# Gate and up tiles from seven half-size products, and the residual summed in DRAM

## The chip, the cores and the metric

The program runs on one core of one Trainium2 chip. The metric is the device time of one execution in microseconds, as the median of several runs. The engines are named as in the profile: PE is TensorE (PEld its weight loads), DVE is VectorE, ACT is ScalarE, POOL is GpSimd, and SP is the engine that issues most DMAs.

## The reference

An encoder of two layers works on 768 tokens (a prompt of 512 and a sample of 256) with 1024 features. Each layer has three parts: a SwiGLU, a mixer (windowed attention and a long convolution), and a second SwiGLU. Each part is modulated by a conditioning vector `c` and closed by a layer norm. Cut to what matters here:

```python
mod = (silu(c) @ ada_w[l] + ada_b[l]).reshape(B, 9, 1024)
h = x * (1 + mod[:, 1]) + mod[:, 0]
g, u = split(h @ wi, 2)                  # wi: 1024 x 5632
f = (silu(g) * u) @ wo                   # wo: 2816 x 1024
x = layer_norm(ALPHA * x + 0.5 * (1 + mod[:, 2]) * f)
```

There are four SwiGLU parts in all: parts 0 and 2 of layer 0 and parts 0 and 2 of layer 1.

## The kernel before

Features lie on the 128 partitions and tokens run along the free axis, so an activation is a set of tiles of 128 features by 768 tokens. Every product is made of three matmuls in fp32r: the operand is split into a high part (a ScalarE copy that rounds) and a low part (a VectorE subtraction), and high x high, high x low and low x high are added up in PSUM (`mm3`, line 393). Weights are split on the fly. They come in units of 128 x 1024 (eight blocks of 128 x 128) in the fixed order of `w_units`: `w_load` (206) issues SP's DMA, `w_ahead` (213) has ScalarE write the high part and VectorE the low part of the next units, up to n ahead, and `w_take` (225) hands the next unit out.

The order of work on each engine is the order of the program text: the schedule is written by hand, an engine runs its instructions in that order, and each instruction waits for its operands and for its output buffer. Buffers come from fixed sets of slots (line 120): `slot_s` for activations, `slot_w` for split weights (6), `slot_r` and `slot_q` for raw weights, `slot_t` for temporaries (6), and eight PSUM banks.

A SwiGLU part (`swiglu`, 570) goes like this. The 2816 hidden features are 22 tiles j, each with a gate unit and an up unit. The first three j (six units) are made in the head, `Proj.head` (422), which overlaps with the layer norm of the part before (`final`, 505; `Norm.apply`, 354): the sample's columns first, then the prompt's. In part 0, where nothing is before, they are plain units. Then `rest` (593) makes j = 3 to 21 one after the other with `one` (598): `Proj.unit` (412) runs, for each of the two units, 24 matmuls of 512 columns and 24 of 256; `done` (578) applies Silu to the gate, multiplies it with the up tile on VectorE and splits the result into an `a` tile. The hidden tiles are consumed in six chunks. After the j named in `UNTIL`, the first four chunks of four hidden tiles each are multiplied with `wo` for all eight output tiles d in `out_step` (480), and VectorE adds each result to the residual x in SBUF. The last two chunks are run by `sample_out` (486) and `final`, interleaved with the norm.

```python
def out_step(o, x, coef, d):
    bp, bs = bank(), bank()
    o.d([(bp[:, :LP], 0), (bs[:, :LS], 1)], d)
    for s, b in ((0, bp[:, :LP]), (1, bs[:, :LS])):
        stt(x(d, SEQ[s]), b, coef[:, d, s:s + 1], x(d, SEQ[s]), ALU.mult, ALU.add)
```

A background generator, `ada_steps` (633), makes the modulation vectors from `ada_w`. One call of `pump(1)` (237) makes one tile: two VectorE passes over 128 x 1024, one for each sequence, and a DMA for a later tile. It runs in layer 0 alone: 56 tiles from the start of part 0, and 72 from the end of the head of part 2. `one` pumps two tiles per j in part 0 and three in part 2; the out steps pump one (part 0) or two (part 2) every second d.

The residual is written to DRAM (`x_spill`) only ahead of a mixer, which reads it back (`spill` in `finish`, `reload` in `attention`, 1333).

## Time and profile before

| | |
|---|---|
| median of 3 runs | 3071.99 us (3071.22 to 3072.28) |
| the profiled execution | 3068.34 us |
| its span, first to last instruction | 3066.5 us |
| mean granted clock of TensorE over the span | 0.989 |
| TensorE busy | 2988.5 us, 97% |
| TensorE weight loads busy | 2611.0 us, 85% |
| VectorE busy | 1754.6 us, 57% |
| ScalarE busy | 985.1 us, 32% |
| GpSimd busy | 456.9 us, 15% |
| DMA | 288.11 MB, mean 94 GB/s |

The profile shows one execution. A line of its timeline has the start in us from the span's start, the duration, the engine, the line of the kernel, the operation, the tiles written and read, their shape, the number of instructions merged into the line, and in brackets the idle time before it with what ended it. All instructions of this kernel go through one helper line (L70), so they are told apart by their tiles and shapes. Matmuls overlap: the duration of one record is longer than the distance between two starts.

### The profile page before, as it was taken

What the parts mean: (1) busy time and instruction counts of PE and PEld (TensorE: products, weight loads), DVE (VectorE), ACT (ScalarE), POOL (GpSimd) and SP (SyncE); (2) the same over time, 40 slices, a digit from 0 to 9 for tenths busy, and PEclk for the clock granted to TensorE, in tenths of its full rate; (3) what the DMA queues carried; (4) which work ended last, traced back from release to release, by engine and by line L of the source; (5) the groups of instructions that cost most, each with busy time, mean ns of one, the idle gap of its engine ahead of it and who ended that gap; (6) DMA issues with size and microseconds to landing.
All of it is one profiled execution on the core that took longest, in us unless ns stands there. A gap on an engine that the chain in (4) does not pass through costs nothing. (4 is left out here: it accounts for less than half of the span.)

```text
span 3066.5 us, 42447 instructions
## 1 busy us (share of the span) xinstructions
PE 2988.5 (97%) x17380; PEld 2611.0 (85%) x17380; DVE 1754.6 (57%) x3064; ACT 985.1 (32%) x1677; POOL 456.9 (15%) x459
## 2 busy tenths in 40 slices
PE   9999999999899999999999999999989999999998
PEld 3788888888888888888888888888888888888888
DVE  5565655567868667788273333325786873233326
ACT  3521112234367522111243111213426752211223
POOL 2400000034432400000040000003443240000002
PEclk9999999999999999999999999999999999999999
DMA  5433333323121145445121111112312111111111
GB/s 200 179 138 138 114 134 124 110 79 121 57 89 42 35 151 172 172 162 175 63 69 54 62 65 62 62 63 76 124 62 69 56 42 62 63 63 66 65 63 56
DMA packets 78571, 288.11 MB, mean 94 GB/s; under 512 B 11223, under 2 KB 14504, under 8 KB 75689
## 3 DMA queue, kind: packets, MB, share of 16 engines
q1 hardware_dynamic: 74680, 258.83, 24.8%
q0 software_dynamic: 3696, 26.58, 2.3%
q8 instruction: 136, 2.23, 0.3%
q14 instruction: 59, 0.48, 0.0%
HBM read 267.55 MB, written 17.83 MB: 93 GB/s over the span
## 5 line engine op out<-in xcount | busy, mean ns | idle before, releaser
L70 PE MATMUL bank<-slot_s,slot_w 128*128 128x512 f32 (+1 forms) x15000 | 2613.4, 336 | 20.2 <-DVE slot_s L70 15.8
L70 PEld LDWEIGHTS bank<-slot_s,slot_w 128*128 128x128 f32 x15000 | 2301.4, 191 | 320.3 <-DVE slot_s L70 21.5
L70 DVE TENSOR_TENSOR slot_w<-slot_r,slot_w 128x1024 fp32r<-128x1024 f32 x282 | 344.8, 1227 | 424.5 <-ACT slot_w L70 424.4
L70 ACT ACTIVATE slot_w<-slot_r 128x1024 fp32r<-128x1024 f32 x316 | 327.2, 1049 | 296.1 <-DMA slot_r<-w_units 244.4
L70 DVE SCALAR_TENSOR_TENSOR slot_s<-bank,tiny,slot_s 128x256 f32<-128x256 f32 (+1 forms) x416 | 238.9, 595 | 202.0 <-PE bank L70 201.9
L70 DVE CUSTOM_DVE_ANT_0 slot_t<-slot_q,slot_q 128x1024 bf16<-128x1024 f32 x256 | 310.8, 1222 | 28.1 <-DMA slot_q<-ada_t 17.3
L70 ACT ACTIVATE slot_t<-bank 128x512 f32<-128x512 f32 (+2 forms) x206 | 103.9, 505 | 679.9 <-PE bank L70 670.0
L70 DVE TENSOR_TENSOR slot_t<-slot_t,bank 128x256 f32<-128x256 f32 (+1 forms) x280 | 151.1, 540 | 272.6 <-PE bank L70 263.5
L70 ACT ACTIVATE slot_s<-slot_t 128x512 fp32r<-128x512 f32 (+1 forms) x220 | 114.8, 529 | 588.6 <-DVE slot_t L70 583.4
L70 POOL COPY slot_t<-slot_s 128x256 f32<-128x256 f32 (+1 forms) x13 | 6.6, 508 | 1984.7 <-DVE slot_s L70 1473.8
L70 DVE TENSOR_TENSOR slot_s<-slot_t,slot_s 128x256 fp32r<-128x256 f32 (+1 forms) x278 | 180.2, 650 | 118.7 <-ACT slot_s L70 104.1
L70 PE MATMUL bank<-slot_w,slot_s 128*128 128x256 f32 x864 | 107.6, 285 | 0.0
L70 PEld LDWEIGHTS bank<-slot_w,slot_s 128*128 128x128 f32 x864 | 105.5, 193 | 0.0
L70 POOL TENSOR_TENSOR slot_t<-slot_t,slot_s 128x256 f32<-128x256 f32 (+1 forms) x91 | 94.5, 1038 | 66.2 <-DVE slot_s L70 61.7
L70 ACT ACTIVATE slot_t<-slot_s 128x256 f32<-128x256 f32 (+1 forms) x132 | 65.6, 509 | 106.2 <-DVE slot_s L70 97.8
L70 POOL TENSOR_TENSOR slot_w<-slot_r,slot_w 128x1024 fp32r<-128x1024 f32 x34 | 81.5, 2399 | 119.4 <-ACT slot_w L70 100.8
L70 PE MATMUL bank<-slot_w,slot_w 128*128 128x256 f32 (+1 forms) x384 | 71.6, 342 | 20.4 <-ACT slot_w L70 14.8
L70 PEld LDWEIGHTS bank<-slot_w,slot_w 128*128 128x128 f32 x384 | 61.0, 215 | 30.1 <-ACT slot_w L70 17.4
L70 DVE TENSOR_TENSOR slot_t<-slot_t,slot_t 128x256 f32<-128x256 f32 (+3 forms) x120 | 78.6, 655 | 6.1 <-ACT slot_t L70 3.9
L70 ACT ACTIVATE slot_w<-slot_w,tiny 128x256 f32<-128x256 f32 (+1 forms) x144 | 74.4, 535 | 9.9 <-DVE tiny L70 9.6
L70 POOL TENSOR_SCALAR slot_s<-slot_t,lnp 128x256 f32<-128x256 f32 (+1 forms) x80 | 59.4, 743 | 83.4 <-DVE slot_t L70 83.0
L70 ACT ACTIVATE slot_s<-slot_t,tiny,tiny 128x256 fp32r<-128x256 f32 (+1 forms) x80 | 56.4, 704 | 46.9 <-DVE slot_t L70 46.9
(120 smaller groups left out, 1459.4 us busy)
## 6 DMA issues: line engine op xcount, KB each, us to landing
slot_r<-w_units SPq DMA_DIRECT2D x316, 512.0 KB, 3.5
slot_q<-ada_t SPq DMA_DIRECT2D x128, 512.0 KB, 3.6
slot_q<-ada_nat SPq DMA_DIRECT2D x16, 512.0 KB, 4.5
g_main<-slot_s POOLq DMA_DIRECT2D x4, 1536.0 KB, 8.7
x_spill<-slot_s POOLq DMA_DIRECT2D x4, 1536.0 KB, 7.0
slot_s<-g_main SPq DMA_DIRECT2D x4, 1536.0 KB, 7.2
slot_s<-x_spill POOLq DMA_DIRECT2D x4, 1536.0 KB, 7.1
slot_s<-x_in SPq DMA_DIRECT2D x2, 1536.0 KB, 9.0
```

Of the source, the lines that this page charges most:

```text
L70: return getattr(real, name)(*args, **kwargs)
```

## The change

The pairs j = 3 to 21 are made in another way. Take a pair's raw weights as a 2 x 2 block matrix: rows are input features 0 to 511 and 512 to 1023, columns are gate and up. Take the activations as 2 x 2 blocks too: the feature halves by tokens 0 to 383 and 384 to 767. The eight block products become seven (the scheme of Strassen and Winograd), each of a sum of weight blocks and a sum of activation blocks, and their results are combined by additions. Each product is 4 x 3 matmuls of 384 columns.

- The class `Fast` replaces `one`. `mid`, called inside the head ahead of the results of the prompt's first four banks (in part 0 after unit 3), makes the activation sums on GpSimd and VectorE, splits them, and loads the raw weights of j = 3. `begin` copies one more sum into h and prepares the first pair. `period` makes one pair and prepares the next.
- `sums` forms four weight sums per pair on GpSimd; per pair seven weight blocks of 128 x 512 are split (`prep_a` to `prep_d`), where it were four (two units of 128 x 1024).
- One bank collects four products; ScalarE copies it between products.
- The raw weights of a fast pair are loaded into a `slot_w`; the rest keep the old path with its own order (`_plan`) and a limit up to which `w_ahead` may split.
- `out_step` becomes `out_add`: ScalarE scales the two banks into a temporary, and a GpSimd DMA adds that to the residual in DRAM. The residual is in `x_spill` from the start of each SwiGLU part (for the first by a DRAM copy of `x_in`) and is read back ahead of the last two chunks.
- `slot_q` and `slot_r` become one set of seven, `slot_s` has ten, and the DMA descriptor scratch is set to 4096.

```diff
-SLOTS = {"slot_s": 9, "slot_w": 6, "slot_r": 3, "slot_q": 4, "slot_t": 6, "bank": 8, "tiny": 12}
+SLOTS = {"slot_s": 10, "slot_w": 6, "slot_r": 7, "slot_t": 6, "bank": 8, "tiny": 12}
...
     def w_ahead(n):
-        while w_state["split"] < min(w_state["next"] + n, n_units):
+        while w_state["split"] < min(w_state["next"] + n, w_state["limit"]):
...
-            w_load(i + 3)
+            w_load(i + w_state["raws"])
...
+            if self.mid is not None:
+                self.mid()
             w_ahead(2)
...
-    def out_step(o, x, coef, d):
+                w_ahead(min(self.ahead, self.room - len(self.ws)))
+    def out_add(o, coef, d):
         bp, bs = bank(), bank()
         o.d([(bp[:, :LP], 0), (bs[:, :LS], 1)], d)
+        v = slot_t([T])
         for s, b in ((0, bp[:, :LP]), (1, bs[:, :LS])):
-            stt(x(d, SEQ[s]), b, coef[:, d, s:s + 1], x(d, SEQ[s]), ALU.mult, ALU.add)
+            act.activation(out=v[:, SEQ[s]], in_=b, func=AF.Copy, scale=coef[:, d, s:s + 1])
+        gp.dma_start(x_spill[:, d, :], v, accum_op=ALU.add)
...
             for ci, chunk in enumerate(CHUNKS):
                 last = ci + 1 == len(CHUNKS)
-                while nj[0] < UNTIL[ci]:
-                    one()
+                while fast.j < UNTIL[ci]:
+                    fast.period(ci < 4 and fast.j + 1 == UNTIL[ci])
                 if coef is None:
                     coef = coef_of(l, 3 * which + 2, 0.5 / ALPHA)
                 o = Out([(a_of(j)[:, 0], a_of(j)[:, 1]) for j in chunk])
                 if ci + 2 >= len(CHUNKS):
+                    if not os:
+                        xn = Feat()
+                        for i in range(2):
+                            gp.dma_start(xn.more(i), x_spill[:, 4 * i:4 * i + 4, :])
+                        w_state["limit"], w_state["raws"] = w_stops.pop(0), 3
                     o.room = 6 - sum(before.n for before in os)
                     os.append(o)
                     if last:
                         drain()
-                        return end(os, x, coef)
+                        return end(os, xn, coef)
                     continue
+                w_state["limit"], o.ahead = w_state["next"] + len(chunk), 1
                 for d in range(ND):
-                    out_step(o, x, coef, d)
+                    out_add(o, coef, d)
...
+        def mid(self):
+            hh, hl = self.hh, self.hl
+            self.tt = {n: slot_s([4, 2, HT], F32R) for n in (2, 3, 4)}
+            self.t1 = slot_s([4, HT])
+            for d in range(4):
+                fa, fb, v = slot_t([2, HT]), slot_t([2, HT]), slot_t([2, HT])
+                al = slice(0, T)
+                tt(fa.rearrange("p a b -> p (a b)"), f32(hh(d, al)), f32(hl(d, al)), ALU.add, eng=gp)
+                tt(fb.rearrange("p a b -> p (a b)"), f32(hh(d + 4, al)), f32(hl(d + 4, al)), ALU.add, eng=gp)
+                tt(self.t1[:, d], fa[:, 0], fa[:, 1], ALU.subtract, eng=gp)
+                tt(v[:, 0], fb[:, 1], fa[:, 1], ALU.subtract)
+                stt(v[:, 1], v[:, 0], -1.0, fa[:, 0], ALU.mult, ALU.subtract)
+                stt(fb[:, 0], v[:, 1], -1.0, fb[:, 0], ALU.mult, ALU.subtract)
+                srcs = ((3, v[:, 0]), (2, v[:, 1]), (4, fb[:, 0]))
+                for n, src in srcs:
+                    acopy(self.tt[n][:, d, 0], src)
+                for n, src in srcs:
+                    tt(self.tt[n][:, d, 1], src, f32(self.tt[n][:, d, 0]), ALU.subtract)
+            self.load(NHEAD)
...
+        def load(self, j):
+            if j in self.place:
+                raw = self.raw[j] = slot_w([2, 2, 512], F32)
+                for i in range(2):
+                    sp.dma_start(raw[:, i].rearrange("p a b -> p (a b)"), w_units[self.place[j] + i])
...
+        def sums(self, j):
+            if j in self.raw:
+                r = self.raw[j]
+                v = self.vs[j] = slot_w([4, 512], F32)
+                tt(v[:, 0], r[:, 1, 0], r[:, 1, 1], ALU.add, eng=gp)
+                tt(v[:, 1], r[:, 0, 0], v[:, 0], ALU.add, eng=gp)
+                tt(v[:, 2], r[:, 0, 0], r[:, 1, 0], ALU.add, eng=gp)
+                tt(v[:, 3], r[:, 0, 1], v[:, 1], ALU.add, eng=gp)
...
+        def product(self, out, j, wn, hn, first, last):
+            wh, wl = self.w.pop((j, wn))
+            for k in range(4):
+                b = slice(k * P, (k + 1) * P)
+                start = first and k == 0
+                mm(out, wh[:, b], self.h(hn, k, 0), start, False, skip_group_check=True)
+                mm(out, wh[:, b], self.h(hn, k, 1), False, False, skip_group_check=True)
+                mm(out, wl[:, b], self.h(hn, k, 0), False, k == 3, skip_group_check=True)
...
+        def p1(self, j):
+            st = self.st[j] = {"b1": bank()[:, :HT], "sg": slot_t([2, HT])}
+            self.product(st["b1"], j, "r11", "h11", True, False)
+            acopy(st["sg"][:, 0], st["b1"])
+        def p2(self, j):
+            st, b3 = self.st[j], bank()[:, :HT]
+            self.product(b3, j, "r12", "h21", True, True)
+            g = st["sg"][:, 0]
+            tt(g, b3, g, ALU.add)
+            act.activation(out=g, in_=g, func=AF.Silu)
+        def begin(self):
+            j = self.j
+            for c in (slice(0, 2), slice(2, 4)):
+                hi, lo = (f.t[0][:, c, HT:] for f in (self.hh, self.hl))
+                acopy(hi, self.t1[:, c])
+                tt(lo, self.t1[:, c], f32(hi), ALU.subtract)
+            w_state["raws"] = 2
+            self.prep_a(j)
+            self.sums(j)
+            self.p1(j)
+            self.prep_b(j)
+            self.p2(j)
+            self.prep_c(j)
+            self.raw.pop(j)
+            self.load(j + 1)
+        def period(self, before_chunk):
+            j, n = self.j, self.j + 1
+            st = self.st[j]
+            b1, sg = st["b1"], st["sg"]
+            self.prep_a(n)
+            self.prep_d(j)
+            self.product(b1, j, "v2", "t2", False, False)
+            acopy(sg[:, 1], b1)
+            pump(1)
+            b2 = bank()[:, :HT]
+            self.product(b2, j, "v1", "t1", True, False)
+            self.sums(n)
+            self.product(b1, j, "v3", "t3", False, False)
+            u = slot_t([HT])
+            acopy(u, b1)
+            tt(u, b2, u, ALU.add)
+            pump(1)
+            self.prep_b(n)
+            if n in self.raw:
+                self.p1(n)
+            self.product(b1, j, "r22", "t4", False, True)
+            stt(sg[:, 0], b1, -1.0, sg[:, 0], ALU.mult, ALU.mult)
+            self.prep_c(n)
+            if n in self.raw:
+                self.raw.pop(n)
+                self.load(n + 1)
+                self.p2(n)
+            if self.which:
+                pump(1)
+            if before_chunk:
+                w_state["limit"] = w_state["next"] + 4
+                w_ahead(1)
+            self.product(b2, j, "v4", "h22", False, True)
+            tt(sg[:, 1], b2, sg[:, 1], ALU.add)
+            act.activation(out=sg[:, 1], in_=sg[:, 1], func=AF.Silu)
+            stt(sg[:, 1], u, -1.0, sg[:, 1], ALU.mult, ALU.mult)
+            a = self.a_of(j)
+            split_to(a[:, 0], a[:, 1], sg.rearrange("p a b -> p (a b)"))
+            self.j = n
...
+    gp.dma_start(x_spill, x_in)
...
-        final(os, norm, nxt[0], 4 if nk == 1 else 6, spill if nk == 1 else None)
+        final(os, norm, nxt[0], 4 if nk == 1 else 2 * NHEAD, spill)
         return nxt
     background.append(ada_steps(0, list(range(16, 72)), 0, cb))
     part = make_part(0, x, h)
-    for i in range(6):
+    for i in range(2 * NHEAD):
         part[0].unit(i)
         pump(1)
+        if i == 3:
+            part[0].mid()
     for i in range(len(PARTS)):
         if i == 2:
```

## Rows read from the trace of the kernel before

**Rows 1.** The page, part 1: busy us (share of the span) and instructions.

```profile
PE 2988.5 (97%) x17380; PEld 2611.0 (85%) x17380; DVE 1754.6 (57%) x3064; ACT 985.1 (32%) x1677; POOL 456.9 (15%) x459
```

**Rows 2.** Windows, layers 0, 1: us; busy PE, PEld, DVE, ACT, POOL; PEclk, DMA, GB/s.

```profile
340.00:400.00 60.00, 60.00 (x343) 52.95 (x342) 33.32 (x51) 12.39 (x19) 0.00 (x0) 1.00 0.37 131
...
2000.00:2100.00 100.00, 100.00 (x600) 89.49 (x599) 33.54 (x49) 22.60 (x33) 0.00 (x0) 1.00 0.21 69
```

**Rows 3.** VectorE's timeline, layer 1 SwiGLU: start us, us, instruction, count, idle before.

```profile
2022.02 0.69 DVE L70 TENSOR_TENSOR slot_t<-slot_t,bank 128x512 f32<-128x512 f32 x1 [2.88 <-PE bank L70]
...
2038.70 0.69 DVE L70 TENSOR_TENSOR slot_t<-slot_t,bank 128x512 f32<-128x512 f32 x1 [2.88 <-PE bank L70]
```

**Rows 4.** TensorE's timeline in three stretches of one shape.

```profile
2091.77 12.40 PE L70 MATMUL bank<-slot_s,slot_w 128*128 128x256 f32 x102
...
929.12 1.58 PE L70 MATMUL bank<-slot_s,slot_s 128*128 128x384 f32 x8
...
1612.65 29.63 PE L70 MATMUL bank<-slot_s,slot_w 128*128 128x512 f32 x130
```

**Rows 5.** Groups of TensorE's instructions by shape: count, busy us, mean ns, idle before.

```profile
L70 PE MATMUL bank<-slot_s,slot_w 128*128 128x512 f32 x7272 | 1721.2, 391 | 4.4 <-DVE slot_w L70 2.9 <-DVE slot_s L70 1.5
L70 PE MATMUL bank<-slot_s,slot_w 128*128 128x256 f32 x7728 | 995.6, 284 | 15.8 <-DVE slot_s L70 14.3 <-DVE slot_w L70 1.5
...
L70 PE MATMUL bank<-slot_s,slot_s 128*128 128x384 f32 x64 | 12.6, 338 | 0.0
```

**Rows 6.** Groups of VectorE's instructions by shape.

```profile
L70 DVE TENSOR_TENSOR slot_w<-slot_r,slot_w 128x1024 fp32r<-128x1024 f32 x282 | 344.8, 1227 | 424.5 <-ACT slot_w L70 424.4
L70 DVE CUSTOM_DVE_ANT_0 slot_t<-slot_q,slot_q 128x1024 bf16<-128x1024 f32 x256 | 310.8, 1222 | 28.1 <-DMA slot_q<-ada_t 17.3 <-ACT slot_q L70 6.0
L70 DVE SCALAR_TENSOR_TENSOR slot_s<-bank,tiny,slot_s 128x512 f32<-128x512 f32 x180 | 134.1, 746 | 134.5 <-PE bank L70 134.5
...
L70 DVE TENSOR_TENSOR slot_t<-slot_t,bank 128x512 f32<-128x512 f32 x128 | 87.5, 684 | 207.7 <-PE bank L70 206.5 <-DVE slot_t L70 0.5
...
L70 DVE TENSOR_TENSOR slot_t<-slot_t,bank 128x256 f32<-128x256 f32 x152 | 63.6, 418 | 65.0 <-PE bank L70 57.0 <-ACT slot_t L70 6.3
```

**Rows 7.** Groups of ScalarE's instructions by shape.

```profile
L70 ACT ACTIVATE slot_w<-slot_r 128x1024 fp32r<-128x1024 f32 x316 | 327.2, 1049 | 296.1 <-DMA slot_r<-w_units 244.4 <-PE bank L70 51.7
L70 ACT ACTIVATE slot_s<-slot_t 128x512 fp32r<-128x512 f32 x116 | 72.6, 631 | 433.5 <-DVE slot_t L70 428.3 <-issue 4.9
L70 ACT ACTIVATE slot_t<-bank 128x512 f32<-128x512 f32 x114 | 68.0, 597 | 499.1 <-PE bank L70 489.3 <-DVE mods L70 9.8
...
L70 ACT ACTIVATE slot_t<-bank 128x256 f32<-128x256 f32 x88 | 33.7, 382 | 180.8 <-PE bank L70 180.7
```

**Rows 8.** VectorE's timeline in the mixer of layer 0.

```profile
768.39 1.78 DVE L70 TENSOR_TENSOR slot_t<-slot_s,slot_s 128x512 f32<-128x512 f32 x1
770.21 1.67 DVE L70 TENSOR_TENSOR slot_q<-slot_q,slot_t 128x512 f32<-128x512 f32 x1
773.04 0.69 DVE L70 TENSOR_TENSOR slot_t<-slot_s,slot_s 128x512 f32<-128x512 f32 x1 [1.17 <-POOL slot_t L70]
```

**Rows 9.** GpSimd's timeline in the same stretch.

```profile
767.88 3.44 POOL L70 TENSOR_TENSOR slot_t<-slot_s,slot_s 128x512 f32<-128x512 f32 x2
771.40 1.60 POOL L70 TENSOR_TENSOR slot_t<-slot_t,slot_t 128x512 f32<-128x512 f32 x1
```

**Rows 10.** Groups of GpSimd's instructions by shape.

```profile
L70 POOL TENSOR_TENSOR slot_w<-slot_r,slot_w 128x1024 fp32r<-128x1024 f32 x34 | 81.5, 2399 | 119.4 <-ACT slot_w L70 100.8 <-issue 18.5
...
L70 POOL TENSOR_TENSOR slot_s<-slot_t,slot_s 128x512 fp32r<-128x512 f32 x22 | 28.3, 1291 | 48.9 <-ACT slot_s L70 46.7 <-DVE slot_t L70 1.8 <-issue 0.4
```

**Rows 11.** GpSimd's timeline, head of layer 1's first SwiGLU.

```profile
1614.56 1.07 POOL L70 TENSOR_SCALAR slot_s<-slot_t,lnp 128x512 f32<-128x512 f32 x1 [1.31 <-DVE slot_t L70]
```

**Rows 12.** VectorE's timeline, end of the same head.

```profile
1641.03 0.69 DVE L70 TENSOR_TENSOR slot_t<-slot_t,bank 128x512 f32<-128x512 f32 x1 [5.56 <-PE bank L70]
```

**Rows 13.** DMA issues: issuing queue, count, KB each, median us to landing.

```profile
x_spill<-slot_s POOLq DMA_DIRECT2D x4, 1536.0 KB, 7.0
```

More of the change, by code (lines that the diff above doesn't have):

```diff
@@ L117, in dram, with _plan @@
         return self.dram_pool.tile(shape, F32, name=name) if self.real else _View(None)
-SLOTS = {"slot_s": 9, "slot_w": 6, "slot_r": 3, "slot_q": 4, "slot_t": 6, "bank": 8, "tiny": 12}
+SLOTS = {"slot_s": 10, "slot_w": 6, "slot_r": 7, "slot_t": 6, "bank": 8, "tiny": 12}
+NHEAD = 3
+HT = T // 2
+def _plan():
+    order, fast, stops, at = [], [], [], 0
+    for _ in range(DEPTH):
+        for part in range(3):
+            if part == 1:
+                order += range(at, at + 26)
+                at += 26
+                continue
+            place, nj = {}, 0
+            for ci, chunk in enumerate(CHUNKS):
+                while nj < UNTIL[ci]:
+                    if nj < NHEAD:
+                        order += [at, at + 1]
+                        if nj + 1 == NHEAD:
+                            stops.append(len(order))
+                    else:
+                        place[nj] = at
+                    at += 2
+                    nj += 1
+                order += range(at, at + len(chunk))
+                at += len(chunk)
+            fast.append(place)
+    return order, fast, stops + [len(order)]
 @with_exitstack
@@ L178, in affine, with mm @@
         act.activation(out=out, in_=a, func=AF.Identity, scale=scale, bias=bias)
[L180 to L181 removed]
+    def mm(out, lhsT, rhs, start, stop, **more):
+        pe.matmul(out, lhsT, rhs, start=start, stop=stop, **more)
     ident = const("ident", [P], F32R)
```

68 lines of the change are left out of this document (50 added, 18 removed).

## The prediction

> **What bounds the kernel now.** I read the engine shares first: TensorE is busy for 2988.5 us of the span of 3066.5 [rows 1]. Then two windows in the SwiGLU stages: TensorE is busy for all of 60 and of 100 us, at granted clock 1.00 (2.4 GHz), while VectorE is at 56% where the background work on the conditioning weights (ada) runs, in layer 0, and at 34% in layer 1; GpSimd is idle in both [rows 2]. VectorE's timeline repeats every 16.68 us, one pair of gate and up tiles [rows 3]. So these stages run at TensorE's pace, and the price of a pair is read from starts of matmuls. Over long runs of one shape [rows 4], less the last record's own length [rows 5], a 512-column matmul takes (29.63 - 0.39)/129 = 0.227 us, a 256-column one (12.40 - 0.28)/101 = 0.120. 48 of each make 16.66: the 16.68 is all matmul.
>
> **What seven products give.** A half-size product is 4 x 3 matmuls of 384 columns. Eight such matmuls in a row took 1.58 us, so (1.58 - 0.34)/7 = 0.177; the middle of the 512 and 256 spacings is 0.1735. I take 0.1755 (ends 0.1735 and 0.1775: 76 periods x 84 x 0.002, 13 us either way). A product takes 2.11, a period of seven 14.74, so a period is worth 1.94. There are 19 per part, j = 3 to 21, four parts: -147 us if everything else stays beside TensorE. It does not.
>
> **The wait inside a period (no ada: layer 1).** v3.t3 adds into the bank that the ScalarE copy after v2.t2 has to read first. That copy stands on ScalarE behind the finish of the period before: VectorE's sum 0.55, Silu 0.5, VectorE's product 0.61, the high part of 768 columns 0.84; then behind the next raw tile's high part 1.05 and the 512-column one 0.63, and takes 0.49 itself [rows 6, 7]; 384 and 768 columns are interpolated between the shapes of the rows. That is 4.67, plus 0.16 until the last matmul's record ends, 4.83. TensorE has two products to cover it, 4.22. The wait is 0.6; I take 0.7, since no hand-over between engines is in the sum. The first period and those after an out chunk have no such finish in front: 14 of 19 have. A layer-1 part gives 19 x 1.94 - 14 x 0.7 = 27, both 54.
>
> **VectorE in layer 0.** Per period it now has low parts of weights 2 x 1.23 + 3 x 0.69 = 4.5, results 3 x 0.55 + 2 x 0.61 + 0.96 = 3.8, and waits of 0.5 and 0.84 for ScalarE in the finish: 9.7. An ada tile is two passes of 1.22 [rows 6]: two pumps (part 0) make 14.5, three (part 2) 17.0. Before, one pair cost VectorE only two weight splits and two results.
> GpSimd now adds four 512-column sums per period. What that does is seen in the mixer: VectorE's additions with both inputs in SBUF, 0.69 alone, last 1.78 and 1.67 while GpSimd adds, and GpSimd's 1.29 becomes 1.7; they end in turn (770.17 VectorE, 771.32 GpSimd) [rows 8 to 10]. One GpSimd addition thus holds VectorE for up to 771.32 - 770.17 = 1.15, four for 4.6. The bounds are 0 (they fall beside VectorE's reads of PSUM and its waits) and 4.6; I take half, 2.3, as VectorE's PSUM reads (2.3) and waits (1.3) can hide some of it. A period then takes VectorE 16.8 in part 0 and 19.3 in part 2, against 14.74 on TensorE.
> The Trainium skill, "SBUF — State Buffer", section "Who interferes with whom", calls this an exclusive lock: a VectorE instruction with two SBUF inputs and a GpSimd instruction that reads SBUF wait for each other in full. The trace agrees, with 1.78 and 1.67 for 0.69 [rows 8, 9]; by the rule in full, with nothing beside PSUM reads, a period would bear the 4.6 and the sum be 71 higher, and the ada passes would wait too, which no row shows.
> In a group of four periods ahead of an out chunk the first starts without a finish (3.5 less), 2.3 late (the last bank copies and a weight copy): 15.6 or 18.1. Three more and the low part of the chunk's first weights, which is queued behind: 15.6 + 3 x 16.8 + 1.2 = 67.2, or 18.1 + 3 x 19.3 + 1.2 = 77.2, against 4 x 16.68 = 66.7. Three groups: +1.5 and +31. The first two periods: 0 and +5. The last five: in part 0 three have ada, 15.6 + 2 x 16.8 + 2 x 15.45 = 80.1 against 83.4, -3; in part 2 none, 14.74 + 4 x 15.45 = 76.5, -7. Part 0: -1. Part 2: +30. All period stages together: -54 - 1 + 30 = -25.
>
> **The new start of a stage.** `mid` makes the four sums of activations: on GpSimd 8 additions of 768 columns (1.85, between 1.29 and 2.40) and 4 of 384 (1.0), 18.8; on VectorE 24 operations of 384, 0.58 each, 14, all with two SBUF inputs. One at a time that is 33; I take 31, since an addition holds the other for 0.13 less than it lasts. It can begin near 1617, when the norm's last GpSimd step (1614.56 + 1.07) [rows 11] and two DMA issues are through, and ends at 1648. TensorE is done with the head at 1640.8: VectorE's read of its last bank starts at 1641.03 [rows 12]. The heads' results are queued behind `mid`: three Silu of 0.6, three products of 0.69 with high parts of 0.63, 5.8; then `begin` copies two pieces of 768 (1.7), and the first weight pair needs 1.05 + 1.23. The first product starts at 1648 + 9.8, 17 us after TensorE fell idle. Before, the next tile stood ready there. Three such starts: 51. In part 0 `mid` comes after unit 3 and only two units (16.7) cover it; VectorE gets to it some 4 late (a result and an ada tile), needs 24 (GpSimd has begun already), then two ada tiles (4.9), the results and `begin` (5): 38 - 16.7 = 21. Together +72. If it all hid, the first weight split would still leave some 5 each.
>
> **The new end.** After the last period no split is queued ahead (`w_ahead` is called there only from `w_take`), so the first weight split of the last two chunks follows the finish: 0.55 + 0.5 + 0.61 + 0.84 + 1.05 + 1.23 = 4.8, and 0.7 for small operations between. 5.5 x 4 = +22; TensorE waits.
>
> **The residual.** VectorE loses two operations per out step (ScalarE takes them at 0.6 and 0.38, in 4.17 us of TensorE); no time there, TensorE had none to wait. The 128 accumulating DMAs of 384 KB, four more spills and reloads lie on GpSimd's queue beside matmuls: a plain 1536 KB write landed in 7.0 [rows 13]. I take 0: each has 4.17 and several buffers; the dear end is a rival. The copy of x into DRAM runs beside the first units: 0.
>
> **Sum**: -25 + 72 + 22 = +69. Against the profiled execution, 3068.34 us (span 3066.5 and 1.8 around it), 3137; the median of the runs is 3.7 higher: **3141**.
>
> **Rivals.**
> (A) Faster: the two engines' additions do not hold each other up; the place is the four sums per period and `mid`. VectorE's period is then 14.5 in part 0, under TensorE's 15.45, and 17.0 in part 2: part 0 -26, part 2 -3, with layer 1 -83. `mid` takes 24 (its own chain through three free buffers) and leaves 10 per start, 40, and the ends 22: -21, 3051. It decides where a GpSimd addition costs VectorE under about a quarter of 1.15. Against it stand [rows 8, 9]; for it, that half of VectorE's work there reads PSUM. 0.27.
> (B) The additions hold each other up, but those of a period fall beside the ada passes, which no row shows next to GpSimd: stages -83, starts 72, ends 22: +11, 3083. By the skill's rule these passes have two SBUF inputs and would wait. 0.14.
> (C) The accumulating DMAs take longer than an out step, 4.17: at 6 us each, 128 x 1.8 = 230 on top, 3370. A quarter of the row's 7.0 speaks against it; that none here adds while it writes, for it. 0.05.
>
> **Numbers.** The forecast's case has 0.48, the rest 0.06 lies about it. A change of under 0.2% (6 us) cannot be told from none here. The range goes from 3035 (A, less the spacing's 13) to 3195 (three quarters of the way to every GpSimd addition holding VectorE in full, 2.3 x 31 periods = 71 more). Faster 0.28 (A), same 0.04, slower 0.68.
>
> **What would show it.** In the profile after: matmuls of 128x384 near 0.175 apart; VectorE above 90% busy in layer 0's stages, with low parts of 0.69 lasting over 1 us beside GpSimd; TensorE idle 10 to 20 us after each head, waiting for weight tiles from VectorE, and 5 before the last chunks; layer-1 periods near 15.4, layer-0 ones 17 to 19. I am wrong if layer-0 periods are under 15.5, if the starts are under 6, or if out chunks are longer than 33.3.

## The result and the profile after

The changed kernel took **3246.02 us** (median of 4 runs, 3242.41 to 3250.66) beside 3071.60 for the kernel before on the same chip: a ratio of 1.0569, 95% interval 1.0551 to 1.0588. It is slower, as forecast, but by 174 us where 69 were forecast; it lies 51 above the end of the range. The profiled execution took 3245.85 (span 3244.1).

Part 1 of the page after, and of its part 2 TensorE's clock in 40 slices (before, all 9):

```profile
PE 2923.2 (90%) x16468; PEld 2645.0 (82%) x16468; DVE 2183.8 (67%) x3292; ACT 1376.5 (42%) x2369; POOL 1193.3 (37%) x954
...
PEclk9979999999999989999999899999999998999998
```

Beside [rows 1]: TensorE has 912 matmuls less, and 65 us less of busy time, yet the span grew. It fell from 97% to 90% busy. VectorE gained 429 us, ScalarE 391, GpSimd 736.

Two windows of layer 0 (part 0, part 2) and one of layer 1, columns as in [rows 2]:

```profile
330.00:390.00 60.00, 52.92 (x278) 48.58 (x277) 41.65 (x54) 24.01 (x38) 17.34 (x12) 0.94 0.52 150
1395.00:1455.00 60.00, 47.81 (x253) 46.53 (x251) 52.41 (x73) 21.34 (x35) 20.73 (x12) 0.94 0.40 142
1886.00:1946.00 60.00, 57.93 (x333) 56.97 (x332) 38.78 (x40) 26.57 (x43) 28.53 (x17) 1.00 0.24 66
```

Against the 60.00 of [rows 2] TensorE is now busy for 53 and 48 of 60 us in layer 0 and for 58 in layer 1. VectorE is at 69% in the window of part 0, which holds 22 us of an out chunk, and at 87% in that of part 2; over four periods without a chunk (from 296.75 and from 1376.49) it is at 87 and 90%.

The streaming itself came as forecast. TensorE's timeline of a period in layer 1:

```profile
1907.27 8.62 PE L70 MATMUL bank<-slot_s,slot_w 128*128 128x384 f32 x48 [0.86 <-ACT slot_t L70]
1915.73 2.28 PE L70 MATMUL bank<-slot_s,slot_r 128*128 128x384 f32 x12
1917.85 4.33 PE L70 MATMUL bank<-slot_s,slot_w 128*128 128x384 f32 x24
1923.04 8.63 PE L70 MATMUL bank<-slot_s,slot_w 128*128 128x384 f32 x48 [0.86 <-ACT slot_t L70]
```

48 matmuls with a last record of 0.34: (8.62 - 0.34)/47 = 0.176 us each, forecast 0.1755. The period is 15.77 against 16.68 [rows 3]: 14.8 of matmuls and a wait of 1.0 ahead of v3 (0.86 here, behind a last record that runs on).

What TensorE waited for, all in all (us, times, longest):

```profile
PE bank L70 <- ACT slot_w L70: 133.2, 29, 26.6
PE bank L70 <- ACT slot_t L70: 86.8, 59, 5.4
PE bank L70 <- DVE slot_w L70: 52.1, 53, 4.8
```

The stages in us, from the matmul that spreads one norm's result (`bank<-ident,tiny`) to that of the next (TensorE's timeline; part 0 from its first 256-column matmul):

```
                 before   after   change   forecast
layer 0 part 0    525.3   601.2    +75.9      +25.5
layer 0 part 2    573.1   649.7    +76.6      +52.5
layer 1 part 0    556.9   569.3    +12.4       -4.5
layer 1 part 2    568.1   578.9    +10.8       -4.5
all the rest      843.1   845.0     +1.9        0
```

VectorE's timeline over one period of part 2 in layer 0 shows what sets it (from one sum after v4 to the next, 21.40 us):

```profile
1397.75 0.55 DVE L70 TENSOR_TENSOR slot_t<-bank,slot_t 128x384 f32<-128x384 f32 x1
...
1401.31 2.28 DVE L70 TENSOR_TENSOR slot_w<-slot_w,slot_w 128x1024 fp32r<-128x1024 f32 x1
1403.52 1.76 DVE L70 TENSOR_TENSOR slot_r<-slot_w,slot_r 128x512 fp32r<-128x512 f32 x1
...
1410.49 1.22 DVE L70 TENSOR_TENSOR slot_w<-slot_w,slot_w 128x1024 fp32r<-128x1024 f32 x1
...
1417.96 1.27 DVE L70 TENSOR_TENSOR mods<-mods,tiny 128x16 f32<-128x16 f32 x1 [1.71 <-DMA tiny<-ada_b]
1419.15 0.54 DVE L70 TENSOR_TENSOR slot_t<-bank,slot_t 128x384 f32<-128x384 f32 x1
```

The low part of 1024 columns lasts 2.28 beside GpSimd's sums and 1.22 away from them, that of 512 columns 1.76 for 0.69. VectorE has next to no idle time but its waits for ScalarE in the finish, and here one for a bias load.

The new start of a stage, layer 1's part 0: TensorE, then GpSimd, then VectorE:

```profile
1784.64 10.73 PE L70 MATMUL bank<-slot_s,slot_w 128*128 128x512 f32 x46
1814.83 1.01 PE L70 MATMUL bank<-slot_s,slot_w 128*128 128x384 f32 x2 [19.45 <-ACT slot_w L70]
...
1770.61 3.65 POOL L70 TENSOR_TENSOR slot_t<-slot_s,slot_s 128x768 f32<-128x768 f32 x2
1778.76 1.07 POOL L70 TENSOR_TENSOR slot_s<-slot_t 128x384 f32<-128x384 f32 x1 [4.50 <-DMA x_spill<-slot_s]
...
1799.11 0.99 POOL L70 TENSOR_TENSOR slot_s<-slot_t 128x384 f32<-128x384 f32 x1
1800.06 1.57 POOL L70 TENSOR_TENSOR slot_w<-slot_w 128x512 f32<-128x512 f32 x1
...
1800.55 3.04 DVE L70 SCALAR_TENSOR_TENSOR slot_t<-slot_t,slot_t 128x384 f32<-128x384 f32 x2
1803.51 3.62 DVE L70 TENSOR_TENSOR slot_s<-slot_t,slot_s 128x384 fp32r<-128x384 f32 x3
```

The four such waits are 26.6, 19.5, 19.5 and 19.7, with 1 to 3 us more behind each. GpSimd's first difference waits 4.50 for the spill of x whose slot it takes, which the forecast did not have.

### The profile page after: what moved, and what is told of

It is laid out like the page before. It is cut to its first block, busy times and chain, and to the rows that moved or that the text cites. A ratio compares the mean times of both kernels' runs of the same rounds, so it can differ in the third digit from the quotient of the medians.

```text
span 3244.1 us, 42484 instructions
## 1 busy us (share of the span) xinstructions
PE 2923.2 (90%) x16468; PEld 2645.0 (82%) x16468; DVE 2183.8 (67%) x3292; ACT 1376.5 (42%) x2369; POOL 1193.3 (37%) x954
## 3 DMA queue, kind: packets, MB, share of 16 engines
q0 software_dynamic: 24208, 102.08, 14.8%
## 5 line engine op out<-in xcount | busy, mean ns | idle before, releaser
L70 PE MATMUL bank<-slot_s,slot_w 128*128 128x384 f32 (+2 forms) x13176 | 2398.4, 342 | 262.3 <-ACT slot_w L70 118.2
L70 DVE TENSOR_TENSOR slot_w<-slot_w,slot_w 128x1024 fp32r<-128x1024 f32 (+1 forms) x304 | 367.4, 1229 | 193.2 <-ACT slot_w L70 193.2
L70 POOL TENSOR_TENSOR slot_w<-slot_w 128x512 f32<-128x512 f32 x152 | 257.4, 1693 | 561.2 <-DMA slot_w<-w_units 384.2
L70 DVE CUSTOM_DVE_ANT_0 slot_t<-slot_r,slot_r 128x1024 bf16<-128x1024 f32 x256 | 344.2, 1350 | 62.2 <-DMA slot_r<-ada_t 25.6
L70 DVE TENSOR_TENSOR slot_w<-slot_r,slot_w 128x1024 fp32r<-128x1024 f32 (+1 forms) x142 | 167.8, 1193 | 232.3 <-ACT slot_w L70 226.1
L70 DVE TENSOR_TENSOR slot_s<-slot_t,slot_s 128x768 fp32r<-128x768 f32 (+3 forms) x250 | 239.3, 968 | 98.2 <-ACT slot_s L70 83.5
L70 POOL TENSOR_TENSOR slot_w<-slot_w,slot_w 128x512 f32<-128x512 f32 x152 | 283.1, 1862 | 6.0
L70 ACT ACTIVATE slot_w<-slot_w 128x1024 fp32r<-128x1024 f32 (+1 forms) x304 | 246.3, 837 | 24.1 <-DVE slot_r L70 24.1
L70 ACT ACTIVATE slot_w<-slot_r 128x1024 fp32r<-128x1024 f32 (+1 forms) x188 | 183.1, 995 | 122.1 <-DVE slot_r L70 114.4
L70 PE MATMUL bank<-slot_s,slot_r 128*128 128x384 f32 x912 | 171.9, 336 | 0.0
L70 DVE SCALAR_TENSOR_TENSOR slot_t<-slot_t,slot_t 128x384 f32<-128x384 f32 (+1 forms) x114 | 94.7, 830 | 46.2 <-ACT slot_t L70 44.9
```

What stands on the lines that cost most here:

```text
L70: return getattr(real, name)(*args, **kwargs)
```

## The experiments

"The changed kernel" is the one above; its own 3246 is compared with each run's median.

**Which work holds VectorE (two runs).** First, ada passes 16 columns wide in place of 1024 (the conditioning sums leave out the other columns):

```diff
-            vec.tensor_tensor_reduce(out=junk, in0=raw, in1=cb[s], scale=1.0, ...
+            vec.tensor_tensor_reduce(out=junk[:, :16], in0=raw[:, :16], in1=cb[s][:, :16], scale=1.0, ...
```

> The two VectorE passes of an ada tile run over 16 columns in place of 1024 (the other columns' sums are left out); all else as in the changed kernel. Theory (in layer 0 VectorE is the bound, by its ada passes on top of the new work): the SwiGLU parts of layer 0 come near those of layer 1 (634 and 638 us against 569 and 574), in all 100 to 125 less, about 3130. Rival (GpSimd's sums hold VectorE up whatever it runs, the ada passes lie beside): under 25 less, over 3220. The four long waits ahead of the first pair stay at 19 to 27 either way.

3138.21 us, ratio 1.0221 (1.02 to 1.0241): 108 less. Part 0 fell to 548.1 and part 2 to 593.6; layer 1 stayed (569.4, 578.3). Without the passes VectorE no longer sets layer 0: four periods of part 0 take 62 to 63 us, as in layer 1, for 70 to 71.

Second, no weight sums on GpSimd (the tile that they fill is filled by two loads):

```diff
-                tt(v[:, 0], r[:, 1, 0], r[:, 1, 1], ALU.add, eng=gp)
...
+                for i in range(2):
+                    sp.dma_start(v[:, 2 * i:2 * i + 2].rearrange("p a b -> p (a b)"), w_units[self.place[j] + i])
```

> GpSimd's four sums per pair are left out; their tile is filled by two more loads of the raw weights. Theory (a GpSimd addition and a VectorE operation with two SBUF inputs exclude each other, so the sums lengthen VectorE's work): VectorE's low parts go back to 0.69 and 1.23 from 1.6 to 2.3, layer 0 gains about 1 us in each of its 31 periods with ada, layer 1 next to nothing (its VectorE has slack): 25 to 45 less in all. Rival (the two engines do not hold each other up where it matters): within 8 of the changed kernel.

3146.77 us, ratio 1.0248 (1.0228 to 1.0269): 99 less, over twice the upper expectation. Part 0 fell to 553.7 and part 2 to 615.7, and layer 1, for which next to nothing was expected, by 10 and 9 (559.3, 569.9). VectorE's groups between 300 and 700 us (count, busy us, mean ns, idle before), first in the changed kernel:

```profile
L70 DVE CUSTOM_DVE_ANT_0 slot_t<-slot_r,slot_r 128x1024 bf16<-128x1024 f32 x84 | 115.0, 1370 | 17.8 <-ACT slot_t L70 11.2 <-DMA x_spill<-slot_t 5.2
L70 DVE TENSOR_TENSOR slot_w<-slot_w,slot_w 128x1024 fp32r<-128x1024 f32 x32 | 57.6, 1800 | 11.8 <-ACT slot_w L70 11.8
L70 DVE TENSOR_TENSOR slot_r<-slot_w,slot_r 128x512 fp32r<-128x512 f32 x17 | 27.9, 1642 | 0.0
...
L70 DVE SCALAR_TENSOR_TENSOR slot_t<-slot_t,slot_t 128x384 f32<-128x384 f32 x17 | 15.0, 883 | 10.1 <-ACT slot_t L70 10.1
```

and in the run without the sums:

```profile
L70 DVE CUSTOM_DVE_ANT_0 slot_t<-slot_r,slot_r 128x1024 bf16<-128x1024 f32 x81 | 98.9, 1222 | 15.7 <-DMA x_spill<-slot_t 9.7 <-ACT slot_t L70 4.5
L70 DVE TENSOR_TENSOR slot_w<-slot_w,slot_w 128x1024 fp32r<-128x1024 f32 x31 | 37.9, 1223 | 10.4 <-ACT slot_w L70 10.4
...
L70 DVE TENSOR_TENSOR slot_r<-slot_w,slot_r 128x512 fp32r<-128x512 f32 x16 | 11.0, 686 | 0.0
L70 DVE SCALAR_TENSOR_TENSOR slot_t<-slot_t,slot_t 128x384 f32<-128x384 f32 x17 | 9.5, 559 | 10.1 <-ACT slot_t L70 10.1
```

The means fall back to those of [rows 6]. The hold-up in this stretch is 32 x 0.58 + 17 x 0.96 + 84 x 0.15 + 17 x 0.32 = 53 us, in 17 periods: **3.1 us a period**, 0.7 of it on the ada passes. The same sum over part 2's periods (1376 to 1684) gives 2.5, 0.6 of it on the passes. The forecast had 2.3, and none on the passes.

**The order on ScalarE:** the bank copy after v2 goes ahead of the next tile's splits.

```diff
-            self.prep_a(n)
-            self.prep_d(j)
             self.product(b1, j, "v2", "t2", False, False)
             acopy(sg[:, 1], b1)
+            self.prep_a(n)
+            self.prep_d(j)
```

> ScalarE's copy of the bank after the first product stands ahead of the two weight splits of the period, not behind them; nothing else changes. Theory (that copy comes 1.0 us late only since it is queued behind two weight splits): the wait ahead of the third product goes in layer 1, 14 x 1.05 x 2 = 29 less there; layer 0 is held by VectorE and gains 0 to 15: 25 to 45 less. Rival (the wait comes from the chain that finishes the pair before): under 8 less.

3218.08 us, ratio 1.0481 (1.046 to 1.0502): 28 less. The wait ahead of v3 is gone from layer 1 (569.3 to 557.1, 578.9 to 566.1), as the forecast's queue on ScalarE had it; layer 0 gained 3 and 2, since VectorE sets it.

**The residual's part alone, on the kernel before:** the output is scaled by ScalarE and added in DRAM, with x copied there at the start and read back; pairs as before.

```diff
-            stt(x(d, SEQ[s]), b, coef[:, d, s:s + 1], x(d, SEQ[s]), ALU.mult, ALU.add)
+            act.activation(out=v[:, SEQ[s]], in_=b, func=AF.Copy, scale=coef[:, d, s:s + 1])
+        gp.dma_start(x_spill[:, d, :], v, accum_op=ALU.add)
...
+    gp.dma_start(x_spill, x_in)
```

> The kernel before with the residual's part alone: out steps scaled by ScalarE and added in DRAM, x copied to DRAM at the start, read back ahead of the last two chunks, spilled after every norm. Theory (only the copy at the start costs: it fills the DMA engines for 20 us, so the first ada tile is late and VectorE splits a weight late behind it): 3 to 10 more than before. Rival (the 128 accumulating DMAs or their queue cost TensorE time): over 25 more.

3078.41 us (8 runs), ratio 1.0026 (1.0015 to 1.0037): 8 more, all in part 0 (525.3 to 534.7); the other three stages stand within 0.7. The 128 adding DMAs cost nothing that shows. The DMA issues of the changed kernel:

```profile
x_spill<-slot_t POOLq DMA_DIRECT2D x128, 384.0 KB, 5.1
...
x_spill<-x_in POOLq DMA_DIRECT2D x1, 23.7
```

5.1 us to landing is longer than an out step, but nobody waits for it at once. The copy is what costs.

**The copy, put early** in the changed kernel (where x is loaded, not just ahead of the first unit):

```diff
         sp.dma_start(x.more(i), x_in[:, 4 * i:4 * i + 4, :])
+    x_spill = mem.dram("x_spill", [P, ND, T])
+    gp.dma_start(x_spill, x_in)
...
-    gp.dma_start(x_spill, x_in)
```

> Edit on the changed kernel: the copy of x into DRAM is issued where x is loaded, before the filters, in place of just before the first unit. Theory (the copy takes all DMA engines for 20 us and makes the first weights and ada tiles late): the wait of 4.9 us near 152 and the late ada tiles go, 6 to 12 us less than the changed kernel, all of it in the first stage. Rival (VectorE is behind by 20 us in that stage anyway): within 4 us.

3237.34 us, ratio 1.0545 (1.0527 to 1.0564): 9 less, part 0 by 10. In the changed kernel the copy landed at 150, when windows show what it pushed aside (after the busy times: granted clock, DMA share, GB/s):

```profile
130.00:140.00 10.00, 10.00 (x57) 8.77 (x56) 0.00 (x0) 3.33 (x4) 0.00 (x0) 1.00 1.00 403
140.00:150.00 10.00, 10.00 (x62) 8.92 (x61) 0.00 (x0) 2.01 (x2) 0.00 (x0) 1.00 1.01 387
150.00:160.00 10.00, 5.24 (x26) 4.23 (x25) 5.48 (x8) 0.91 (x2) 2.75 (x1) 0.86 0.67 235
```

All DMA engines are taken. VectorE waits 25.6 us for its first ada tile (17.3 in the kernel before), and then TensorE 4.8 for weights.

**The end of a stage:** the last chunks' first split also goes ahead of the last finish.

```diff
-                w_state["limit"] = w_state["next"] + 4
+                w_state["limit"] = w_state["next"] + (4 if before_chunk < 2 else 3)
                 w_ahead(1)
...
-                    fast.period(ci < 4 and fast.j + 1 == UNTIL[ci])
+                    fast.period((1 if ci < 4 else 2) if fast.j + 1 == UNTIL[ci] else 0)
```

> Edit on the changed kernel: the first weight split of the last two out chunks is also queued ahead of the last period's finish, as it is ahead of the other chunks. Theory (the wait at the end of each stage, 3.8 + 1.3 us in layer 1, comes of that split alone): the four waits go, 15 to 22 us less than the changed kernel, near 3226. Rival (VectorE has no time for the split there, and the last period becomes longer by as much): within 6 us of the changed kernel.

3227.38 us, ratio 1.0511 (1.0495 to 1.0528): 19 less, 4 to 6 in each stage. The forecast's term of 22 was close.

**The start of a stage:** four pairs by eight products in place of three, the first chunk ahead of the first period, and `begin`'s work between that chunk's steps; two weight units are also split amid `mid`.

```diff
-NHEAD = 3
+NHEAD = 4
...
-UNTIL = tuple(c[-1] + 2 for c in CHUNKS[:-2]) + (NF, NF)
+UNTIL = (4,) + tuple(c[-1] + 2 for c in CHUNKS[1:-2]) + (NF, NF)
...
                 for d in range(ND):
                     out_add(o, coef, d)
...
+                    if ci == 0 and d > 0:
+                        next(start, None)
```

> Edit on the changed kernel: the fourth pair of a SwiGLU stage is made by eight products too, and the first out chunk runs before the first period of seven; the preparation of the first seven-product pair is put between the out steps of that chunk. Theory (the 20 to 29 us at each stage's start are VectorE's and GpSimd's sums with nothing for TensorE to do beside them): the four waits, 90 us together, nearly go; four pairs cost 1.9 us more each, and the chunk may wait some 3 us for the fourth pair's results; 55 to 80 us less than the changed kernel, layer-1 stages 14 to 18 us less each. Rival (VectorE is full over the whole of a layer-0 stage, so that what is saved at its start comes back as waits in its periods): layer 1 gains 30 to 36 in all, layer 0 under 10.

3162.72 us, ratio 1.0303 (1.0287 to 1.0319): 83 less, 18 to 24 in every stage, layer 0's among them. So the starts were the price of work with no cover, and full VectorE did not take the gain back.

**The clock.** After many of layer 0's waits of 2 to 5 us the granted clock is 1.2 GHz for a while, and matmuls of 384 columns stand 0.32 us apart in place of 0.176. Such records cost TensorE some 46 us in layer 0's two SwiGLU stages, where before they cost 2. Did that lengthen the path? Extra matmuls into an unused bank, just ahead of v3:

```diff
+                for k in range(12):
+                    mm(b4, wh[:, :P], self.h("h22", 0, 0), k == 0, k == 11, skip_group_check=True)
             self.product(b1, j, "v3", "t3", False, False)
```

> Edit on the changed kernel: in layer 0 every period but the first of a stage has twelve extra 384-column matmuls (2.1 us) into an unused bank just ahead of the product v3, where TensorE waits 2 to 5 us; nothing else changes. Theory (half-clock stretches of 3.4 us after those waits lengthen the path, 1.4 us each): half of layer 0's stretches go, mean granted clock back to 0.965 to 0.975, and 12 to 30 us less than the changed kernel. Rival (VectorE sets the end of these periods, so that slow matmuls only eat into the next wait): the clock rises as much and the time stays within 8 us, or grows by up to 15 where waits are shorter than 2.1 us.

3263.6 us, ratio 1.0625 (1.0608 to 1.0642): 18 more. They read v4's tile, which itself came late (28 waits for it, the longest 5.1), so the run decides little. With v1's tile, which is there:

```diff
+                m = 18 if self.which else 12
+                for k in range(m):
+                    mm(b4, wd[:, :P], self.h("t1", 0, 0), k == 0, k == m - 1, skip_group_check=True)
```

> Edit on the changed kernel: as the first try with extra matmuls, but these read the tile of v1, which is always there, so that they start as soon as v1 is done and lie inside the wait ahead of v3 (the first try's read v4's tile, which often came later and lengthened the wait). In layer 0, every period but a stage's first: 12 extra in part 0 (2.1 us), 18 in part 2 (3.1 us). Theory (the slow matmuls after the waits are on the path, 1.4 us for each stretch): part 0 8 to 16 us shorter than the changed kernel's 601, part 2 5 to 16 shorter than 650, the total 12 to 30 less. Rival (VectorE sets these periods' ends): the clock rises, the total stays within 8 us.

3262.74 us, ratio 1.0629 (1.0611 to 1.0647): 17 more. In part 0 18 times 2.1 us of matmuls were added, the clock recovered half (records at the lower level cost some 10 us in place of 22), and the stage went from 601.2 to 598.1, where the theory had 8 to 16 less. In part 2 the extra matmuls took more than the waits held, 663.0 for 649.7, which decides nothing there. So in part 0's periods a TensorE that is kept fast gained 3 us: VectorE sets them, and the lower clock is there a sign of the waits. The out chunks, where TensorE sets the pace, the extra matmuls did not reach. One of part 0 and one of layer 1 in the changed kernel:

```profile
474.19:509.98 35.79, 35.47 (x192) 30.36 (x193) 16.45 (x23) 13.05 (x20) 6.08 (x7) 0.95 0.80 178
1949.05:1983.41 34.36, 33.83 (x192) 29.54 (x193) 6.86 (x7) 12.95 (x20) 6.08 (x7) 1.00 0.71 136
```

The same 192 matmuls keep TensorE busy for 1.6 us more at a mean granted clock of 0.95 than at 1.00.

**The edits together** (start, order, end, copy):

> Edit on the changed kernel: the four edits so far together (fourth pair by eight products with the first chunk ahead of the periods; bank copy ahead of the splits; first weight split of the last chunks ahead of the last finish; early copy of x). Theory (they remove different waits): the gains add up, 83 + 28 + 19 + 9 = 139 less than the changed kernel, 3095 to 3125; layer-1 stages near 533 and 545, below the 557 and 568 of the kernel before, layer-0 stages still above theirs. Rival (VectorE is full in layer 0, so that gains there overlap): 3125 to 3150.

3117.44 us, ratio 1.0154 (1.0138 to 1.0169): 129 less of the 139 that they gave one by one. Layer 1 is now 534.7 and 544.6, under the 556.9 and 568.1 of before; layer 0 is 561.2 and 628.8, above its 525.3 and 573.1.

**The ada tiles out of the periods**, into the out chunks, and 40 of layer 1's 72 into layer 1's own part 0:

```diff
-                        pump(2 if which else 1)
+                    pump(int(d > 1) if ci == 0 else 1 + (d % 4 == 0))
...
-            background.append(ada_steps(1, list(range(72)), 56, cb))
+            background.append(ada_steps(1, list(range(32)), 56, cb))
+        if i == 3:
...
+            background.append(ada_steps(1, list(range(32, 72)), 88, cb))
```

> Edit on the combination: the ada tiles leave the periods (12 of them stay, one in a period, in part 0) and go into the out chunks, ten to a chunk, and 40 of layer 1's 72 are made in the chunks of layer 1's part 0 in place of layer 0's part 2; up to two tiles share one scratch tile. Theory (periods in layer 0 are too long for VectorE alone by the ada tiles, while VectorE is idle in the chunks): layer-0 stages come down to some 20 us below the kernel before, as layer 1's do, the layer-1 stages stay; 2975 to 3020, under the kernel before. Rival (VectorE does not get ten tiles into a chunk beside its weight splits, or each tile waits for its load and its scratch tile): chunks longer than 33.3 us, 3030 to 3080.

3074.41 us (10 runs), ratio 1.0017 (1.0007 to 1.0026): 43 less than the combination, but 54 over the upper end of the expectation. It lies in the rival's range, though not for the rival's reason: the chunks with ada tiles take 34.4 to 34.7, as layer 1's did in the changed kernel, and part 0 loses its time in the periods. Part 2 of layer 0 fell by 72; layer 1's part 0, with its 40 tiles, rose by 17, and layer 0's part 0 by 10 to 571.0. VectorE's, GpSimd's and TensorE's timelines there:

```profile
303.01 2.31 DVE L70 CUSTOM_DVE_ANT_0 slot_t<-slot_r,slot_r 128x1024 bf16<-128x1024 f32 x1
305.36 2.17 DVE L70 CUSTOM_DVE_ANT_0 slot_t<-slot_r,slot_r 128x1024 bf16<-128x1024 f32 x1
307.46 2.27 DVE L70 TENSOR_TENSOR slot_w<-slot_w,slot_w 128x1024 fp32r<-128x1024 f32 x1
...
304.20 2.25 POOL L70 TENSOR_TENSOR slot_w<-slot_w 128x512 f32<-128x512 f32 x1
306.41 2.25 POOL L70 TENSOR_TENSOR slot_w<-slot_w,slot_w 128x512 f32<-128x512 f32 x1
...
309.79 2.43 PE L70 MATMUL bank<-slot_s,slot_w 128*128 128x384 f32 x8 [4.13 <-DVE slot_w L70]
```

Where the one ada tile left in a period fell beside GpSimd's sums, each pass took 2.2 to 2.3 for its 1.22, the sums 2.25 for 1.29, and TensorE waited 4.13 for the tile split last.

**The sums on VectorE**, in that version:

```diff
-                tt(v[:, 0], r[:, 1, 0], r[:, 1, 1], ALU.add, eng=gp)
+                tt(v[:, 0], r[:, 1, 0], r[:, 1, 1], ALU.add)
```

(and the other three alike.)

> Edit on that one: the four sums of weights in a period go from GpSimd to VectorE (2.8 us there). Theory (a period's sums on GpSimd hold VectorE for 3.3 us in all): VectorE's busy time per period falls by some 0.5 us and the sums are ready earlier; 5 to 15 us less than the version with the sums on GpSimd. Rival (the sums fall in front of VectorE's results in its queue and hold up the bank that v3 needs): 10 to 40 us more.

3004.80 us, ratio **0.9788** (0.9773 to 0.9803): 70 less, faster than the kernel before. Part 0 went from 571.0 to 521.5. The expectation of 5 to 15 was far too small. VectorE's busy time fell by only 18 us (2143.0 to 2125.2), so its length alone is not the price. There was a second suspect: the sums' own 7 us on the way from a tile's load to its splits. Two runs were to tell.

The same edit alone, in the changed kernel:

> Edit on the changed kernel, and the only one: the four sums of a period run on VectorE (4 x 0.69 = 2.8 us). Theory H (they cost what they hold VectorE, 3.3 us a period): 0.5 us less in some 31 periods of layer 0, 5 to 20 us less than the changed kernel. Theory L (their own 7 us stand on the way from the load to the split): 40 to 80 us less. A rival to both (VectorE, full in layer 0, gets 2.8 more in its queue): 20 to 60 us more.

3190.01 us, ratio 1.0392 (1.0378 to 1.0406): 56 less, in the range of theory L and not in that of H. Each start is 4 us shorter (15.4 for 19.5 in layer 1; 3.04 and 3.62 of VectorE's rows above, at 1800 and 1803, were held by the first pair's sums), the wait ahead of v3 in layer 1 falls from 1.0 to 0.5, and the rest is in layer 0's periods.

And, in the version with the sums on VectorE, four sums more per period on GpSimd that nobody reads:

```diff
+                spare = slot_t([512])
+                for a, b in ((r[:, 1, 0], r[:, 1, 1]), (r[:, 0, 0], r[:, 0, 1])) * 2:
+                    tt(spare, a, b, ALU.add, eng=gp)
                 tt(v[:, 0], r[:, 1, 0], r[:, 1, 1], ALU.add)
```

> Edit on the version with the sums on VectorE (3004.8): GpSimd makes four sums of the same size from the same tile in every period too, into a scratch tile that nobody reads. Theory H (the hold-up of VectorE is what costs): 45 to 70 us more, most of it in part 0 of layer 0. Theory L (the way from the load to the split is what costs): under 25 us more.

3111.07 us, ratio 1.0136 (1.0119 to 1.0152): **106 more**, for work whose result is not used. Part 1 of the page without those sums, and with them:

```profile
PE 2868.1 (96%) x16516; PEld 2607.3 (87%) x16516; DVE 2125.2 (71%) x3560; ACT 1368.9 (46%) x2351; POOL 667.0 (22%) x650
```

```profile
PE 2906.9 (93%) x16516; PEld 2631.8 (85%) x16516; DVE 2329.0 (75%) x3560; ACT 1360.7 (44%) x2351; POOL 1164.2 (37%) x938
```

VectorE runs the same 3560 instructions and is busy for 204 us more, 2.8 in each of the 72 periods. The hold-up alone brings back TensorE's waits for a split tile in part 0 (44.9 us; 44.0 in the version with the sums on GpSimd, 12.1 with them on VectorE), with the way from load to split untouched. It costs more than the 70, and more than theory H had; here VectorE makes the sums as well.

The totals speak for L in one run and for H in the other. The tile that is waited for decides for part 0. The 4.13 above stands ahead of the low part of `r11`, the next pair's first weight block. It is raw: no sum goes into it. TensorE at the same place with the sums on VectorE, and with the unread sums beside them:

```profile
299.84 6.19 PE L70 MATMUL bank<-slot_s,slot_w 128*128 128x384 f32 x34 [0.63 <-DVE slot_w L70]
...
315.20 8.39 PE L70 MATMUL bank<-slot_s,slot_w 128*128 128x384 f32 x34 [4.02 <-DVE slot_w L70]
```

In part 0 such waits make 38 us with the sums on GpSimd, 6 with them on VectorE, and 38 with the unread ones beside. So what counts is where the hold falls: GpSimd's sums lengthen the ada passes ahead of that low part and the low part itself, while VectorE's own sums are queued behind it. The other stages' share of the 70, 20 us, and the share of the two suspects in the 56 were not separated.

**Two last repairs:** layer 1's ada tiles 36 to 36, and in part 0 two more units split amid `mid`.

```diff
-            part[0].mid()
+            part[0].mid(4)
...
-            background.append(ada_steps(1, list(range(32)), 56, cb))
+            background.append(ada_steps(1, list(range(36)), 56, cb))
...
-            background.append(ada_steps(1, list(range(32, 72)), 88, cb))
+            background.append(ada_steps(1, list(range(36, 72)), 92, cb))
```

> Edit on the version with the sums on VectorE: layer 1's ada tiles are divided 36 to 36 in place of 32 to 40 (a part has room for 36 in its chunks; the rest stood at its end), and in the first part two more weight units are split amid the sums of activations. Theory (the waits of 11 us at the end of layer 1's part 0 and of 13 us at the first chunk come of these): 15 to 24 us less, 2980 to 2990, against 3071 and 3246. Rival (VectorE has no room and the waits go elsewhere): within 5 us of 3004.8.

**2989.24 us** (5 runs), ratio **0.9735** (0.9721 to 0.9748): 16 less again, 81 under the kernel before. The wait at the end of layer 1's part 0 went (545.2 to 532.9). At the first chunk 5 us went (521.5 to 516.8) where 13 were hoped for. The two other stages rose by 1 and 2.5. Its SwiGLU stages take 516.8, 548.4, 532.9 and 543.3, 8 to 25 us each under those of before. TensorE's timeline through a period and into a chunk of layer 1 there:

```profile
1909.39 2.28 PE L70 MATMUL bank<-slot_s,slot_r 128*128 128x384 f32 x12
1911.51 12.71 PE L70 MATMUL bank<-slot_s,slot_w 128*128 128x384 f32 x72
1924.06 2.28 PE L70 MATMUL bank<-slot_s,slot_r 128*128 128x384 f32 x12
1926.38 0.73 PE L70 MATMUL bank<-slot_s,slot_w 128*128 128x512 f32 x2
```

From v4 to v4 it is 14.67 us without a wait: the 14.74 of the prediction. In layer 1 the seven products are thus worth what they were priced at, once VectorE is not in their way.

## Why the prediction came out too low

**Right:** the direction and its reason (VectorE with GpSimd beside it in layer 0, sums without cover at each start); the spacing, 0.176 for 0.1755; the end, 19 for 22 when it was taken out; the adding DMAs at nothing, so that rival C fell. Rivals A and B fell too: the engines' additions do hold each other up, and the ada passes are held as well (1370 ns for 1222, up to 2.31 us in a row above).

**Wrong, by size:** the places that add up to the 105 us between 69 and 174 are these.

- "I take half, 2.3" for GpSimd's hold on VectorE, and the ada passes at their undisturbed 1.22. Measured: 3.1 a period in part 0, 0.7 of it on the passes, and 2.5 in part 2. Four periods took 70 to 71 us in part 0 and 77 to 79 in part 2, where 67.2 and 77.2 were forecast: 10 and 3 us in the three groups of each stage. In part 2 waits for bias loads, 1.71 in the row above, are among them.
- The out chunk, 33.3, of which the prediction said that it would be wrong if it were longer. The three behind those groups took 35.4 to 36.2 in part 0 and 35.1 to 36.8 in part 2: 7 and 8 us. All but one ran in part at the lower clock, after a wait for their first weights; what that costs is in the windows above.
- "The first two periods: 0 and +5". They start with `begin`'s splits and the ada tiles still in VectorE's queue. The 192 matmuls from there to the first chunk took 50.0 and 46.4 us in layer 0, 38.2 in layer 1, 33.8 being pure; with the longer chunk behind, some 16 and 7 us over the forecast, and 5 in each of layer 1.
- The start, 21 and 17: 29 and 20 to 21, so 8 and three times 4. The wait of 4.50 for the spill was missing, and so was the hold by the first pair's four sums, 4 us in the run without them. GpSimd's queue now spills x in these stages and then, as its next work, writes a slot that the spill still reads.
- The copy of x, "0": 10 in part 0. A row of the kernel before speaks against the 0, since the DMA engines were full there without the copy, at a share of 0.98:

```profile
130.00:140.00 10.00, 10.00 (x57) 8.77 (x56) 0.00 (x0) 2.26 (x3) 0.00 (x0) 1.00 0.98 374
```

- The wait ahead of v3, 0.7: 1.0, since the finish in front of it is held by GpSimd too (0.5 when the sums are on VectorE). With 1 us more in each chunk (34.4 for 33.3), some 7 us in either layer-1 part.

Of the signs that the prediction named, the low parts over 1 us and the idle starts came. VectorE was not above 90% in layer 0: 87 and 90% over four periods.

The first term was mis-sized for a reason that can be followed. I counted VectorE's PSUM reads and waits as cover for GpSimd's sums. But the sums start when a tile has landed and its split begins, so that they fall beside the two low parts of weights, the ada pass and the finish's product, all with two inputs in SBUF.

The Trainium skill, "SBUF — State Buffer", section "Who interferes with whom", has the two wait for each other in full. Single rows agree (2.28 and 2.31 for 1.22), and the ada passes wait as that rule of the Trainium skill says. Over a period the measured 3.1 is two thirds of the 4.6 that the prediction estimated for four sums in full. By that estimate the forecast would have been 71 higher, 3212, nearer to the 3246 but still short, as the starts, the copy, the chunks and the first periods lie outside it.

## What to carry to other kernels

Before work is given to an idle GpSimd, see which of VectorE's instructions will stand beside it and who waits for these: four sums of 1.3 us cost VectorE 3 us a period, part of it ahead of the split that TensorE needs next, and moving them to VectorE, at 2.8 and behind that split, made the kernel 70 us faster. A saving on the engine that bounds the kernel is only had where every other engine's period stays below its new one; here the seven products paid once the background work had moved to stretches where VectorE was idle. New preparation at a stage's start needs cover of its own length: giving back one pair of the saving (1.9 us) and running a chunk first bought 20.

## What the runs showed of the hardware that was not expected

- Two-input custom passes of VectorE are held by GpSimd as ordinary additions are: 2.31 us for 1.22.
- Idle-looking work is not free: sums that nobody reads cost 106 us of 3005.
- A DMA that adds 384 KB into DRAM landed in 5.1 us, while plain writes of four times that took 7.0; 128 of them beside matmuls cost nothing that could be told.
- A DRAM-to-DRAM copy of 3 MB took 23.7 us at a DMA share of 1.00; the ada tile beside it was waited for 8 us longer than in the kernel before.
- Waits of 2 to 5 us on TensorE were followed by matmuls at the lower clock, but in part 0's periods, which VectorE sets, filling the waits gained 3 us; in an out chunk, which TensorE sets, the slower matmuls took 1.6 us more.
